# A later transpose of the gate, and other PSUM banks for two products of the output projection

## The chip, the cores and the metric

The kernel runs on one core of one Trainium2 chip, in one launch. The metric is the device time of an execution in microseconds (us). Three runs of the kernel before took 2272.88, 2274.70 and 2276.16 us; their median is 2274.7 us.

The engines are named as the profile names them: PE is TensorE (matmuls and transposes), PEld its weight loads, ACT is ScalarE, DVE is VectorE, POOL is GpSimd, and SP is the queue that issues most loads. PSUM, into which TensorE writes, has eight banks here, each a tile of 128 x 512 f32 values.

## The reference

One decoder block for 512 tokens of width 2048, in f32, batch 1:

```
mod = silu(c) @ w_ada + b_ada              # 2048 -> 6 x 2048
shift1, scale1, gate1, shift2, scale2, gate2 = split(mod, 6)
h = rms_norm(x, norm1_w) * (1 + scale1) + shift1
aq, ak, av, gq, gf, gi, gg = split(h @ w_in)      # seven times 1024 columns
attn = rms_norm(dilated_attention(rope(norm(aq)), rope(norm(ak)), av))   # 8 heads, 3 branches
hg   = rms_norm(hgrn2(gq, gf, gi)) * silu(gg)     # 8 heads of a gated linear recurrence
x = x + gate1 * (concat(attn, hg) @ w_out)        # w_out is 2048 x 2048
h2 = rms_norm(x, norm2_w) * (1 + scale2) + shift2
x = x + gate2 * (square(relu(h2 @ w_ff1)) @ w_ff2)   # 2048 -> 8192 -> 2048
```

## The kernel before

Every large matmul is done with numbers split into a high and a low part: `hi` and `lo` of the activations, `whi` and `wlo` of the weights. ScalarE casts the weights `wraw` to `whi` (L39), VectorE subtracts to get `wlo` (L40), and TensorE does three matmuls of 128 x 512 for each pair of tiles (`tok_mm`, L201 to L203, with tokens on the output's partitions; `ch_mm`, L209 to L211, with channels there).

A **product** is 512 columns of a projection. It holds four banks `prj`, one for each 128 rows of output, and runs over 16 slices of 128 of the inner dimension, so it has 16 steps of 12 matmuls. The input projection is a row of such products (`project`, about 180 to 800 us), the output projection has four (`project_out(q)`, q from 0 to 3, about 800 to 990 us). After a product ScalarE copies its four banks out: `gg` of the last product of the input projection at L711, in `hg_gate`; `x1` of the output projection at L944, in `residual`.

PSUM is one pool with two tags of four banks each, `bg` and `mm`: `bank(name, tag="bg")`. A tile gets a bank of its tag that has been given back, and waits for the instruction that reads the former tile last.

Small work is put between the matmul steps by generators. `tick()` takes one step of the list `tasks`: attention, the recurrence, and the turning of their results. `bg_step()` takes one step of the background list `bgw`, 1.85 of them for each step of a product of the input projection. The background work is the modulation `mod`: a step loads `araw`, 128 rows and 512 columns of `w_ada` (L125), and VectorE sums it up with the weights `sc` into `acc` (L129, L131); after the last load of 512 columns TensorE turns the sum into a column (`pc`, L151) and ScalarE reads that out (L154). `mod_rows(2, gate1)` does so for the four quarters of gate 1, lets `lag` background steps pass, turns the columns `gcol` into rows with one transpose (`pr`, L182), copies them (`row`, L184) and writes them to memory (L185), from where `gate1_bc` reads them (L914) after product 1. Behind it in the list stand the eight parts of scale 2 and shift 2 (`mod_cols`).

Attention of a head, in `attention`: `heads_t` turns queries and keys (`ptq`, L458); `scores` (`pscore`, L472, and on VectorE L478 to L481); `weights_t` turns the weights (`pT`, L494); `values` (`po`, L505), which VectorE reads out in four pieces (L509). Values of one head and scores of the next follow each other directly on TensorE. All these tiles, and `pc`, `pr` and the ones below, take banks of tag `bg`.

The output projection needs the results with channels on partitions. `to_mix` turns one head (`ptm`, four transposes of 128 x 128, L553), ScalarE reads it out with a weight (`mix`, L555), and `split_mix` splits that into `hi` (ScalarE, L242) and `lo` (VectorE, L243). In product 1 these run just ahead of the matmuls that need them. In products 2 to 4 and behind, `x1_transposed` turns the new `x1` (`pt2`, L931).

TensorE's order is the order in which the program is written from the input projection's third group on (`manual_schedule`). The order of the other engines is set by a scheduler with its own estimates of durations; a load or a copy marked high priority is put ahead.

Of the kernel before, what the change touches and what calls it, by code (L numbers as in the profile page):

```python
# [19 lines left out]
NT = S // P  # L20
# [24 lines left out]
def hybrid_block(ctx, tc, x, c, positions, norm1_w, w_ada, b_ada, w_in, q_norm_w, k_norm_w,  # L45
# [22 lines left out]
    def bank(name, tag="bg"):  # L68
        return ps.tile([P, 512], F32, name=name, tag=tag)
# [92 lines left out]
    def mod_cols(kind, b, dst, nw, n=512, early=False):  # L162

        for _ in gemv(ada_v, sc, kind * D + b * n, n, early):
            yield
        nb = n // P
        d = dst[:, b * nb:(b + 1) * nb]
        yield from to_cols(gemv.acc, d)
        dve.tensor_tensor(d, d, bcol[:, kind * NK + b * nb:kind * NK + (b + 1) * nb], op=ALU.add)
        if nw is not None:  # L170
            mod_cols.last = dve.scalar_tensor_tensor(d, d, 1.0, nw[:, b * nb:(b + 1) * nb], op0=ALU.add, op1=ALU.mult)
        yield

    def mod_rows(kind, dst, lag=3):

        col = gcol
        for b in range(4):
            yield from mod_cols(kind, b, col, None)
        for _ in range(lag):
            yield  # L180
        pr = bank("pr")
        pe.transpose(pr[0:NK, 0:P], col, ident)  # L182
        row = work("row")
        act.copy(row[0:NK, 0:P], pr[0:NK, 0:P])  # L184
        nc.sync.dma_start(dst.rearrange("o (r p) -> (o r) p", p=P), row[0:NK, 0:P])  # L185
        yield

    def load_w(view, k0, c0, n=512, eng=None, ahead=True, raws=None, behind=False):
        with tc.high_priority() if ahead else ExitStack():
            raw = wr.tile([P, 2, n], F32, name="wraw", tag="raw", bufs=4)  # L190
            with tc.issue_after(marks[-3].ins) if behind else ExitStack():
                nc.sync.dma_start(raw, view[:, k0:k0 + 2, c0:c0 + n])
            if raws is not None:
                raws[:] = [raw[:, 0], raw[:, 1]]
            return [_split(nc, wr, raw[:, j], n, eng if j else None) for j in range(2)]

    def tok_mm(banks, hi, lo, whi, wlo, first, last):

        for ti in range(NT):
            ts = slice(ti * P, (ti + 1) * P)  # L200
            pe.matmul(banks[ti], lhsT=hi[:, ts], rhs=whi, start=first, stop=False)  # L201
            pe.matmul(banks[ti], lhsT=hi[:, ts], rhs=wlo, start=False, stop=False)  # L202
            pe.matmul(banks[ti], lhsT=lo[:, ts], rhs=whi, start=False, stop=last)  # L203
# [30 lines left out]
    def work(name, dt=F32):  # L234
        return wk.tile([P, 512], dt, name=name, tag="wk")
# [113 lines left out]
    def bg_step():  # L349

        while bgw:
            try:
                return next(bgw[0])
            except StopIteration:
                bgw.pop(0)
# [3 lines left out]
    def tick(n=1):  # L359

        for _ in range(n):
            while tasks:
                try:
                    next(tasks[0])
                    break
                except StopIteration:
                    tasks.pop(0)
# [24 lines left out]
    def split_mix():  # L392

        if len(mixp) == NK or mix[korder[len(mixp)]] is None:
            return False
        mixp.append(pair(len(mixp)))
        split_to(mixp[-1], mix[korder[len(mixp) - 1]])
        return True
# [334 lines left out]
    later = []  # L733
    gate1 = dr.tile([1, D], F32, name="gate1")
    gate2 = dr.tile([1, D], F32, name="gate2")
    later.append(mod_rows(2, gate1))
    for b in range(4):
        later.append(mod_cols(4, b, g2c, n2c))
        later.append(mod_cols(3, b, s2c, None))
# [135 lines left out]


    def project_out(q, rate, after):
        banks = [bank("prj", tag="bg" if q % 2 and i < 2 else "mm") for i in range(4)]
        for i0 in range(0, NK, 2):
            for j, (whi, wlo) in enumerate(load_w(wout_v, korder[i0], q * 512)):  # L880
                i = i0 + j
                while q == 0 and len(mixp) <= i:
                    if not split_mix():
                        tick()
                while q == 0 and split_mix():
                    pass
                tok_mm(banks, *mixp[i], whi, wlo, i == 0, i == NK - 1)
                tick(2 if q == 0 and i < 10 else 1)
                owed[0] += rate
                while owed[0] >= 1.0:  # L890
                    bg_step()
                    owed[0] -= 1.0
                after(i)
        return banks

    def nothing(i):
        pass

    banks = project_out(0, 0, nothing)
    while tasks:  # L900
        tick()
# [38 lines left out]
    def residual(q, banks):  # L940
        qs_ = slice(q * 512, (q + 1) * 512)
        with tc.high_priority():
            for ti in (2, 3, 0, 1) if q % 2 else range(NT):
                act.copy(x1[ti][q], banks[ti])  # L944
        for ti in range(NT):
            t = x1[ti][q]
            dve.tensor_tensor(t, t, gate1_bc[:, qs_], op=ALU.mult)
            dve.tensor_tensor(t, t, xin[ti], op=ALU.add)
            act.activation(xin[ti], t, AF.Square, accum_out=ss2[:, ti, q:q + 1])
            pool.dma_start(x1d[:, ti, qs_], t)  # L950

    for q in range(4):
        xin = []
        for ti in range(NT):
            t = xr.tile([P, 512], F32, name="xin", tag="x")
            act.dma_start(t, x_t[:, ti, q * 512:(q + 1) * 512])
            xin.append(t)
        if q:
            banks = project_out(q, 1.7, u_split if q == 3 else nothing)
        residual(q, banks)  # L960
        tasks.append(x1_transposed(q, "bg" if q < 3 else "mm"))
# [221 lines left out]
    def product(i, src, c, ws, tag, by_tile, nxt):  # L1183


        banks = [bank("f2", tag=tag) for _ in range(2)]
        fh, fl = operand(src, c, i)
        ahead = []

        def mm(u, whi, wlo, ts_):  # L1190
            for a in range(2):
                for t in ts_:
                    ts = slice(t * P, (t + 1) * P)
                    first, end = u + a == 0, u + a == KG
                    pe.matmul(banks[t], lhsT=fh[u][a][:, ts], rhs=whi[:, a], start=first, stop=False)  # L1195
                    pe.matmul(banks[t], lhsT=fh[u][a][:, ts], rhs=wlo[:, a], start=False, stop=False)  # L1196
                    pe.matmul(banks[t], lhsT=fl[u][a][:, ts], rhs=whi[:, a], start=False, stop=end)  # L1197

        if by_tile:
            for t in range(2):  # L1200
                for u in range(KG):
                    mm(u, *ws[u], (t,))
        else:
            for u in range(KG):
                mm(u, *ws[u], range(2))
                if u == KG - 1 or src is hparts:
                    tick()
                if nxt and u < KG - 1:
                    ahead.append(nxt(u))
        return banks, ahead  # L1210
# [49 lines left out]
    def after(cs):  # L1260

        return {1: cs[5], 5: cs[6], 6: cs[1], 7: cs[7]}
# [78 lines left out]
    for item, following in zip(items, items[1:] + [None]):  # L1341
        stage_, blk, j, i = item
# [13 lines left out]
        if stage_ == 1:  # L1356
            banks, ahead = product(i, hparts, 0, ws, "bg" if first and j < 2 else "mm", False, call)
# [10 lines left out]
        else:  # L1368
            q, c = blk
            banks, ahead = product(i, fparts, c, ws, "mm", i == 2 and c == NC - 1, call)  # L1370
# [49 lines left out]
def _program(arrays):  # L1420
    import concourse.bacc as bacc
    nc = bacc.Bacc("TRN2", target_bir_lowering=False, num_devices=1)
    args = [nc.dram_tensor(n, a.shape, mybir.dt.from_np(a.dtype), kind="ExternalInput").ap()
            for n, a in arrays.items()]
    args.append(nc.dram_tensor("out_0_dram", _OUTS[0][0], F32, kind="ExternalOutput").ap())
    with tile.TileContext(nc, schedule_with_timeline_sim=True) as tc:
        hybrid_block(tc, *args)
    return nc
# [10 lines left out]
```

## Time and profile before

| | us |
|---|---|
| median of three runs | 2274.7 |
| the profiled execution | 2273.89 |
| its span, from the first to the last instruction | 2272.1 |
| TensorE busy with matmuls | 2219.7 |
| VectorE, ScalarE, GpSimd busy | 1809.6, 1097.3, 441.8 |

Matmuls are pipelined: one of 128 x 512 lasts 0.39 us in the trace, and the next one starts about 0.23 us after it. A row of the rows in time has the start in us from the span's start, the duration in us, the engine, the line, the operation, what it writes and reads, and in brackets the idle time of its engine before it, with what ended it. Several instructions of a kind that follow each other are one row, with their count. A row of waits has the engine and line that waited, what it waited for, and then the total in us, the number of times and the longest.

### The profile page before, as it was taken

What the parts mean: (1) busy time and instruction counts of PE and PEld (TensorE: products, weight loads), DVE (VectorE), ACT (ScalarE), POOL (GpSimd) and SP (SyncE); (2) the same over time, 40 slices, a digit from 0 to 9 for tenths busy, and PEclk for the clock granted to TensorE, in tenths of its full rate; (3) what the DMA queues carried; (4) which work ended last, traced back from release to release, by engine and by line L of the source; (5) the groups of instructions that cost most, each with busy time, mean ns of one, the idle gap of its engine ahead of it and who ended that gap; (6) DMA issues with size and microseconds to landing.
All of it is one profiled execution on the core that took longest, in us unless ns stands there. A gap on an engine that the chain in (4) does not pass through costs nothing.

```text
span 2272.1 us, 33110 instructions
## 1 busy us (share of the span) xinstructions
PE 2219.7 (98%) x11769; PEld 1821.1 (80%) x11769; DVE 1809.6 (80%) x2765; ACT 1097.3 (48%) x1950; POOL 441.8 (19%) x664
## 2 busy tenths in 40 slices
PE   4899999999999999999999999999999999999999
PEld 3788778888778888888887888888888888888887
DVE  6999878768786575678658988998897779967878
ACT  5555434443454464457544555565564333443332
POOL 1000022000220000003232323323232222222221
PEclk9999999999999999999999999999999999999999
DMA  9799454646555266747879789879889987998884
GB/s 324 255 335 336 139 177 150 214 149 211 170 178 160 71 227 202 267 120 264 322 280 361 274 306 385 297 290 377 319 294 378 358 310 263 349 347 310 305 295 164
DMA packets 262583, 598.32 MB, mean 263 GB/s; under 512 B 23220, under 2 KB 43968, under 8 KB 262416
## 3 DMA queue, kind: packets, MB, share of 16 engines
q1 hardware_dynamic: 186800, 332.54, 43.6%
q0 software_dynamic: 70720, 254.21, 30.4%
q10 hardware_dynamic: 4896, 9.44, 1.2%
q8 instruction: 93, 1.52, 0.3%
q14 instruction: 74, 0.61, 0.1%
HBM read 518.49 MB, written 77.61 MB: 262 GB/s over the span
## 4 chain that ended last, share of the span: by engine, by line
PE 70%; DMA 10%; DVE 8%; issue 8%; POOL 2%; ACT 1%; SPq 0%; POOLq 0%; DVEq 0%; ACTq 0%
PE f L1197 9%; PE f L1196 9%; PE f L1195 9%; PE prj L201 8%; PE prj L203 8%; PE prj L202 8%; DMA araw<-in_w_ada_dram 3%; PE f L211 2%; PE f L209 2%; PE f L210 2%; DVE vlo L1180 2%; DMA f_lod<-fs 2%; DVE raw L1163 2%; PE prj L209 1%; PE prj L210 1%
## 5 line engine op out<-in xcount | busy, mean ns | idle before, releaser
L1179 ACT CAST vhi<-raw 128x1024 fp32r<-128x1024 f32 x392 | 413.5, 1055 | 534.1 <-PE f L1197 419.4
L1180 DVE TENSOR_TENSOR vlo<-raw,vhi 128x1024 fp32r<-128x1024 f32 x392 | 476.3, 1221 | 150.8 <-ACT vhi L1179 150.0
L1196 PE MATMUL f<-vlo,Fh 128*128 128x512 f32 x1376 | 537.1, 390 | 3.4 <-DVE vlo L1180 3.3
L1197 PE MATMUL f<-vhi,Fl 128*128 128x512 f32 x1376 | 535.8, 389 | 0.5 <-DMA Fl<-f_lod 0.5
L1195 PE MATMUL f<-vhi,Fh 128*128 128x512 f32 x1376 | 536.1, 390 | 0.0
L39 ACT CAST whi<-wraw 128x512 fp32r<-128x512 f32 (+1 forms) x368 | 219.8, 601 | 445.9 <-PE prj L203 309.7
L201 PE MATMUL prj<-whi,hi 128*128 128x512 f32 x896 | 363.5, 406 | 1.3 <-ACT gg L711 1.3
L203 PE MATMUL prj<-whi,lo 128*128 128x512 f32 x896 | 350.6, 391 | 0.0
L202 PE MATMUL prj<-wlo,hi 128*128 128x512 f32 x896 | 350.0, 391 | 0.6 <-DVE wlo L40 0.6
L40 DVE TENSOR_TENSOR wlo<-wraw,whi 128x512 fp32r<-128x512 f32 (+1 forms) x368 | 243.3, 666 | 115.3 <-ACT whi L39 109.5
L131 DVE SCALAR_TENSOR_TENSOR acc<-araw,sc,acc 128x512 f32<-128x512 f32 (+1 forms) x392 | 254.0, 674 | 99.8 <-DMA araw<-in_w_ada_dram 98.6
L1196 PEld LDWEIGHTS f<-vlo,Fh 128*128 128x128 f32 x1376 | 258.3, 188 | 62.3 <-DVE vlo L1180 8.9
L1197 PEld LDWEIGHTS f<-vhi,Fl 128*128 128x128 f32 x1376 | 258.3, 188 | 54.2 <-DMA Fl<-f_lod 0.9
L1195 PEld LDWEIGHTS f<-vhi,Fh 128*128 128x128 f32 x1376 | 258.3, 188 | 53.7
L1163 DVE TENSOR_TENSOR raw<-raw,raw 128x1024 f32<-128x1024 f32 x224 | 268.3, 1218 | 3.5 <-DMA raw<-in_w_ff_dram 3.1
L203 PEld LDWEIGHTS prj<-whi,lo 128*128 128x128 f32 x896 | 168.1, 188 | 36.6 <-DVE lo L243 0.3
L201 PEld LDWEIGHTS prj<-whi,hi 128*128 128x128 f32 x896 | 168.3, 188 | 36.4 <-ACT gg L711 1.6
L202 PEld LDWEIGHTS prj<-wlo,hi 128*128 128x128 f32 x896 | 168.6, 188 | 33.5 <-DVE wlo L40 1.7
L1141 POOL DMA_DIRECT2D Fh<-f_hid x112 | 79.0, 705 | 424.0 <-PE f L1197 410.3
L211 PE MATMUL f<-hi,wlo 128*128 128x512 f32 x256 | 99.9, 390 | 1.2 <-DVE wlo L40 1.2
L209 PE MATMUL f<-hi,whi 128*128 128x512 f32 x256 | 100.3, 392 | 0.0
L210 PE MATMUL f<-lo,whi 128*128 128x512 f32 x256 | 99.6, 389 | 0.0
(311 smaller groups left out, 2912.0 us busy)
## 6 DMA issues: line engine op xcount, KB each, us to landing
raw<-in_w_ff_dram SPq DMA_DIRECT2D x224, 512.0 KB, 10.1
araw<-in_w_ada_dram SPq DMA_DIRECT2D x384, 256.0 KB, 4.3
Fh<-f_hid POOLq DMA_DIRECT2D x112, 512.0 KB, 6.7
Fl<-f_lod POOLq DMA_DIRECT2D x112, 512.0 KB, 7.8
wraw<-in_w_in_dram SPq DMA_DIRECT2D x104, 512.0 KB, 4.4
Fh<-h_hid POOLq DMA_DIRECT2D x60, 512.0 KB, 6.4
Fl<-h_lod POOLq DMA_DIRECT2D x60, 512.0 KB, 7.4
f_hid<-part POOLq DMA_DIRECT2D x48, 512.0 KB, 8.0
```

Of the source, the lines that this page charges most:

```text
L39: nc.scalar.copy(hi, src)
L40: (eng or nc.vector).tensor_tensor(lo, src, hi.bitcast(F32), op=ALU.subtract)
L131: dve.scalar_tensor_tensor(acc, raw[:, k - k0], vec[:, k:k + 1], acc, op0=ALU.mult, op1=ALU.add)
L201: pe.matmul(banks[ti], lhsT=hi[:, ts], rhs=whi, start=first, stop=False)
L202: pe.matmul(banks[ti], lhsT=hi[:, ts], rhs=wlo, start=False, stop=False)
L203: pe.matmul(banks[ti], lhsT=lo[:, ts], rhs=whi, start=False, stop=last)
L1163: dve.tensor_tensor(dst, a, b, op=ALU.subtract)
L1179: cast_done.append(act.copy(hi, src))
L1180: split_done.append(dve.tensor_tensor(lo, src, hi.bitcast(F32), op=ALU.subtract))
L1195: pe.matmul(banks[t], lhsT=fh[u][a][:, ts], rhs=whi[:, a], start=first, stop=False)
L1196: pe.matmul(banks[t], lhsT=fh[u][a][:, ts], rhs=wlo[:, a], start=False, stop=False)
L1197: pe.matmul(banks[t], lhsT=fl[u][a][:, ts], rhs=whi[:, a], start=False, stop=end)
```

## The change

Two edits, and a third that goes with the second. The lag between the columns of gate 1 and their transpose is six background steps, not three. The products that take two of their banks from tag `bg` are those with even q (the first and the third), not those with odd q. The copies out of the banks are written in the order of the token tiles for all products, where those of odd q had the order 2, 3, 0, 1.

```diff
@@ -733,7 +733,7 @@
     gate1 = dr.tile([1, D], F32, name="gate1")
     gate2 = dr.tile([1, D], F32, name="gate2")
-    later.append(mod_rows(2, gate1))
+    later.append(mod_rows(2, gate1, 6))
@@ -875,7 +875,7 @@
     def project_out(q, rate, after):
-        banks = [bank("prj", tag="bg" if q % 2 and i < 2 else "mm") for i in range(4)]
+        banks = [bank("prj", tag="bg" if q % 2 == 0 and i < 2 else "mm") for i in range(4)]
@@ -940,7 +940,7 @@
         with tc.high_priority():
-            for ti in (2, 3, 0, 1) if q % 2 else range(NT):
+            for ti in range(NT):
                 act.copy(x1[ti][q], banks[ti])
```

How this moves the instructions, at three places. First, TensorE in the input projection, at the transpose `pr` of gate 1 behind the scores of the second head (a piece of the difference):

```order
 L472 MATMUL pscore<-qT 128x128
 L472 MATMUL pscore<-qT 128x256
-L182 MATMUL pr<-ident,gcol 16x128
 L209 MATMUL prj<-hi_1018,whi 128x512
 L210 MATMUL prj<-lo_1019,whi 128x512
 L211 MATMUL prj<-hi_1018,wlo 128x512
+L182 MATMUL pr<-ident,gcol 16x128
 L209 MATMUL prj<-hi_1122,whi 128x512
```

The transpose stands one step of twelve matmuls later. Eight groups of `pc` behind it have moved by one or two steps as well.

Second, one of these groups, in the attention of the last four heads. On TensorE it stood behind the `ptq` before these values and scores, and stands now directly behind the scores. On VectorE, these rows led up to the reading of the values (L509) before:

```order
L131 SCALAR_TENSOR_TENSOR acc<-araw,sc,acc 128x512
L171 SCALAR_TENSOR_TENSOR g2c<-g2c,cols 128x4
L131 SCALAR_TENSOR_TENSOR acc<-araw,sc,acc 128x512 x2
L40 TENSOR_TENSOR wlo<-wraw,whi 128x512
L131 SCALAR_TENSOR_TENSOR acc<-araw,sc,acc 128x512
L509 TENSOR_SCALAR aq<-po,lsum 128x128 x4
```

and these do now:

```order
L40 TENSOR_TENSOR wlo<-wraw,whi 128x512
L481 TENSOR_SCALAR m<-m 128x1 x2
L507 RECIPROCAL lsum<-lsum 128x4
L40 TENSOR_TENSOR wlo<-wraw,whi 128x512 x5
L509 TENSOR_SCALAR aq<-po,lsum 128x128 x4
```

The sums `acc` of the background (L131) have moved away from this place.

Third, TensorE at the beginning of product 1 of the output projection, with what each instruction waits for; before:

```order
L201 MATMUL prj<-whi,hi_8701 128x512 [waits Activation_49]
L202 MATMUL prj<-wlo,hi_8701 128x512
L203 MATMUL prj<-whi,lo_8702 128x512
L553 MATMUL ptm<-ident,gg 128x128 [waits PE_49]
L553 MATMUL ptm<-ident,gg 128x128 x7
L553 MATMUL ptm<-ident,aq 128x128 [waits PE_49]
L553 MATMUL ptm<-ident,aq 128x128 x3
L201 MATMUL prj<-whi,hi_8728 128x512 [waits Activation_49]
```

and now:

```order
L201 MATMUL prj<-whi,hi_8701 128x512 [waits Activation_49]
L202 MATMUL prj<-wlo,hi_8701 128x512
L203 MATMUL prj<-whi,lo_8702 128x512
L553 MATMUL ptm<-ident,gg 128x128 [waits PE_49]
L553 MATMUL ptm<-ident,gg 128x128 x3
L553 MATMUL ptm<-ident,gg 128x128 [waits PE_49]
L553 MATMUL ptm<-ident,gg 128x128 x3
L553 MATMUL ptm<-ident,aq 128x128 [waits Activation_49]
L553 MATMUL ptm<-ident,aq 128x128 x3
L201 MATMUL prj<-whi,hi_8728 128x512
```

The order is the same, the banks are others: the product's first two tiles are in two `bg` banks, and the transposes `ptm` take turns on the other two, so that the third group waits for ScalarE's reading of the first. On ScalarE, the reading of the third group (`mix`, L555) has moved behind the next `hi` (L242) and the next `sg` (L715).

## The prediction

> **What bounds the kernel now.** I read the page's busy times and clock first, then the waits of TensorE, then the stretches of the program that the change touches, then the rows of time around each wait in them.
>
> ```profile
> PE 2219.7 (98%) x11769; PEld 1821.1 (80%) x11769; DVE 1809.6 (80%) x2765; ACT 1097.3 (48%) x1950; POOL 441.8 (19%) x664
> PEclk9999999999999999999999999999999999999999
> ```
>
> TensorE is busy for 2219.7 of 2272.1 us, and its clock is granted in full. A change can only give back TensorE's idle time, 52 us in all, and the next view says where that lies.
>
> ```profile
> PE pc L151 <- DVE acc L131: 12.9, 3, 11.9
> PE ptx L286 <- ACT xs L280: 12.4, 1, 12.4
> PE prj L209 <- ACT hi L339: 6.9, 3, 4.1
> PE pr L182 <- DVE aq L509: 1.6, 1, 1.6
> PE prj L201 <- ACT gg L711: 1.3, 1, 1.3
> ```
>
> The three large waits stand before 100 us, where the change moves nothing. Two small ones are in its reach: the transpose `pr` of gate 1 (1.6 us) and the first matmul of the output projection (1.3 us). Between them, and behind them, this is how full the engines are (busy time with the number of instructions for PE, PEld, DVE, ACT and POOL, then the granted clock and DMA):
>
> ```profile
> 460.00:780.00 320.00, 320.00 (x2365) 260.90 (x2364) 237.60 (x548) 136.01 (x397) 34.10 (x55) 1.00 0.52 161
> 780.00:820.00 40.00, 38.67 (x194) 31.93 (x194) 26.90 (x61) 28.14 (x57) 1.01 (x1) 1.00 0.32 99
> 820.00:990.00 170.00, 169.43 (x784) 139.63 (x783) 110.18 (x177) 75.66 (x162) 6.59 (x12) 1.00 0.70 231
> ```
>
> From 460 to 780 us TensorE has no idle time at all: whatever is reordered there can gain nothing, and can only use up slack. So the most that the change can bring is 1.6 + 1.3 us.
>
> **Part 1: `pr` three steps later.** It is one transpose, one ScalarE copy and one DMA of gate 1's row, and every later background step (the loads `araw`, the sums `acc`, the transposes `pc`) moves behind it by three steps.
>
> ```profile
> 439.63 2.32 PE L472 MATMUL pscore<-qT 128*128 128x512 f32 x8
> 441.66 0.75 DVE L131 SCALAR_TENSOR_TENSOR acc<-araw,sc,acc 128x512 f32<-128x512 f32 x1 [0.55 <-DMA araw<-in_w_ada_dram]
> 442.33 1.12 DVE L509 TENSOR_SCALAR aq<-po,lsum 128x128 f32<-128x128 f32 x4
> 443.50 0.28 PE L182 MATMUL pr<-ident,gcol 128*16 128x128 f32 x1 [1.55 <-DVE aq L509]
> 443.54 0.48 PE L209 MATMUL prj<-hi,whi 128*128 128x512 f32 x1
> ```
>
> The scores end at 439.63 + 2.32 = 441.95. `pr` needs a bank that the values product `po` has held, and VectorE reads it out until 442.33 + 1.12 = 443.45. The order now puts twelve matmuls ahead of `pr`. Twelve matmuls take 2.86 us (800.84 to 803.70 below), so `pr` is reached at about 444.8, over 1 us after its bank is free. The 1.55 us go: **-1.55**. Its copy and its DMA come 3 us later, and that row is read back only when product 1 is over:
>
> ```profile
> L914 SPq DMA_DIRECT2D gate_bc<-gate x4: 319/374/977, 837.0 to 841.8; - x4
> ```
>
> That costs nothing.
>
> What moves with it: eight groups of `pc` come one or two matmul steps later. The only one that comes to stand where `pr` stood, right behind values and scores, is that of the next head group:
>
> ```profile
> 711.90 2.39 PE L505 MATMUL po<-av,p_sb 128*128 128x128 f32 x20
> 712.10 0.62 ACT L39 CAST whi<-wraw 128x512 fp32r<-128x512 f32 x1 [0.77 <-PE prj L203]
> 714.13 2.32 PE L472 MATMUL pscore<-qT 128*128 128x512 f32 x8
> 714.39 0.68 DVE L40 TENSOR_TENSOR wlo<-wraw,whi 128x512 fp32r<-128x512 f32 x1
> 715.13 0.75 DVE L131 SCALAR_TENSOR_TENSOR acc<-araw,sc,acc 128x512 f32<-128x512 f32 x1
> 715.80 1.12 DVE L509 TENSOR_SCALAR aq<-po,lsum 128x128 f32<-128x128 f32 x4
> 716.10 0.59 PE L201 MATMUL prj<-whi,hi 128*128 128x512 f32 x1
> ```
>
> With the group gone from ahead of this place TensorE is 0.35 us earlier, at its scores' end near 715.7. Were VectorE to read `po` out when it does now, until 716.92, `pc` would wait 1.2 us: the wait of part 1 would only have moved. But its order has changed too: the sums `acc` that stood around this point have moved on, and the four reads stand directly behind a `wlo`. That `wlo` needs a `whi` that is cast from about 711.8 on, and so ends near 713; `po` itself ends near 714 (711.90 + 2.39 less 0.35). The reads then run to about 714 + 1.12 = 715.1, ahead of 715.7. I take **0**, with 0 and +1.2 as the bounds. The other moves of loads, casts and sums fall in the stretch without idle time, and there the weights are ready well ahead:
>
> ```profile
> ACT whi L39 <- PE prj L203: 309.7, 154, 6.5
> ```
>
> Here the cast of the next weights waits for TensorE to give a buffer back, 154 times: ScalarE is ahead, not behind. **0**.
>
> **Part 2: banks of the output projection.** Product 1 now takes two banks of tag `bg`, so its first six matmuls need not wait until `gg` has been copied out of the four `mm` banks. TensorE, then ScalarE, around that place:
>
> ```profile
> 798.91 0.60 PE L553 MATMUL ptm<-ident,gg 128*128 128x128 f32 x4
> 800.84 0.50 PE L201 MATMUL prj<-whi,hi 128*128 128x512 f32 x1 [1.33 <-ACT gg L711]
> 803.70 1.03 PE L553 MATMUL ptm<-ident,gg 128*128 128x128 f32 x8
> 804.57 0.60 PE L553 MATMUL ptm<-ident,aq 128*128 128x128 f32 x4
> 804.92 0.48 PE L201 MATMUL prj<-whi,hi 128*128 128x512 f32 x1
> 807.77 1.04 PE L553 MATMUL ptm<-ident,aq 128*128 128x128 f32 x8
> 808.56 0.48 PE L201 MATMUL prj<-whi,hi 128*128 128x512 f32 x1
> 811.59 1.04 PE L553 MATMUL ptm<-ident,aq 128*128 128x128 f32 x8
> ```
>
> ```profile
> 800.21 2.04 ACT L711 COPY gg<-prj 128x512 f32<-128x512 f32 x4
> 802.62 1.19 ACT L715 ACTIVATE sg<-gg 128x512 f32<-128x512 f32 x2
> 803.89 0.62 ACT L39 CAST whi<-wraw 128x512 fp32r<-128x512 f32 x1
> 804.42 1.26 ACT L555 ACTIVATE mix<-ptm,cols 128x512 f32<-128x512 f32 x2
> 806.60 0.69 ACT L555 ACTIVATE mix<-ptm,cols 128x512 f32<-128x512 f32 x1
> 809.26 1.27 ACT L555 ACTIVATE mix<-ptm,cols 128x512 f32<-128x512 f32 x2
> 815.43 0.63 ACT L39 CAST whi<-wraw 128x512 fp32r<-128x512 f32 x1 [0.83 <-PE prj L203]
> ```
>
> Four transposes hold TensorE for 0.35 us (804.57 to 804.92), so the product could begin at 798.91 + 0.35 = 799.26 and not at 800.84: **-1.58**. Its third bank is reached 1.5 us later, at 800.8, just when the first copy of `gg` ends (800.21 + a quarter of 2.04 = 800.7, plus some 0.1): no new wait there.
>
> But the price stands one step on. Three groups of transposes (`ptm`) follow the first twelve matmuls back to back. Before, four banks served them; now the product holds two for its whole length and they take turns on two, so the third group needs the first one's bank. Walking it: the product begins at 799.26, its twelve matmuls end at 802.12, two groups take 0.87 (803.70 to 804.57) to 802.99. The first is read out by ScalarE's `mix` at 804.42, and ScalarE is not free earlier by much: copies, then `sg` until 802.62 + 1.19 = 803.81, then the `whi` cast, which today starts at 803.89 as its buffer comes free and could start at about 803.75. So `mix` runs from 804.28 to 804.28 + 0.68 = 804.96 (the single one at 806.60 took 0.69), and the third group starts there, ends at 805.31, where today the next matmul starts at 804.92. The new wait is 804.96 - 802.99 = **+1.97**; part 2 sums to 1.97 - 1.58 = **+0.39**. Bounds: with ScalarE exactly as now, `mix` ends at 805.10 and the sum is +0.53; with no new wait it is -1.58.
>
> From there on the two banks suffice: each later step has one pair of transposes, and the pair of 807.77 is read out by 809.26 + 1.27 = 810.53, 1.06 us before the next pair begins at 811.59, so I take 0, with what rival D says as the upper end.
>
> Products 2 to 4: no TensorE idle time stands at their starts, so nothing can be gained, and the copies are early enough in either order of banks:
>
> ```profile
> 895.21 2.63 ACT L944 COPY x<-prj 128x512 f32<-128x512 f32 x4
> ```
>
> Copies follow the last matmuls of their banks; the last ends at 897.84, while the next product begins near 897.2 and reaches its third bank 1.5 us and its fourth 2.2 us later. The edit of the order in `residual` moves nothing: in the built programs the copies stand as token tile 0, 1, 2, 3 in both. Product 3 shares the other two `bg` banks with the turned tiles `pt2` as product 2 does today without a wait. **0**.
>
> **Sum.** -1.55 + 0 + 0.39 + 0 = -1.16 us. Span 2272.1 becomes 2270.9, and with the 1.8 us around it the profiled execution's 2273.9 becomes 2272.7. That execution was 0.8 us under the median of the runs, so the forecast for the median is 2274.7 - 1.2 = **2273.5**.
>
> **Rivals.** B: the new wait at the third transposes does not come. For it speaks that ScalarE's `mix` may be put off only by casts that the scheduler places; against it, that its order there is unchanged up to that `mix`. Then -1.55 - 1.58: 2271.6. C: the wait of part 1 comes back at the `pc` of 715 us. For it: the same three things stand in the same order as at 443 us. Against: the sums moved away from ahead of the reads. Price +1.2: 2274.7. D, the other side: ScalarE falls behind on the two banks. One `mix` has moved behind an `hi` cast and an `sg`, 1.05 us later in its queue, and if each of the next four pairs of transposes waits about 1 us for its bank, 4 us are added: 2277.5. It decides once a pair is read out more than the roughly 1 us of slack late; against it speaks that ScalarE has caught up by 815.43, where it waits 0.83 us for TensorE. E: the granted clock falls. The 1.33 us idle time in 780 to 820 left it at 1.00, and a wait of 1.97 us is not much longer.
>
> The Trainium skill (TensorE: Matmul & The Clock Gate, on psum-queue depth-cycling) tells of a kernel that cycled through PSUM banks with small idles and lost its full clock again and again, which speaks against two banks in turn. By its half rate the 192 matmuls of this product, at 0.24 us each, would take some 46 us more, and the time would be about 2320. The trace so far does not bear it out, since the clock stood at 1.00 through the stretch that holds the wait of 1.33 us.
>
> **How the numbers follow.** Chances: the forecast 0.58, B 0.12, C 0.15, D 0.09, E and things not named 0.06. The likeliest's own range, with the spread of the runs (2272.9 to 2276.2), is 2271.8 to 2275.3. The stated range reaches down past B and up to D: 2270.4 to 2277.3. 0.2% is 4.5 us, about what a measurement of this kernel can tell from no change. Neither B (-3.1) nor D (+2.8) reaches it, so only the last case and the outer edge of D or B do: faster 0.05, same 0.89, slower 0.06.
>
> **What would show it.** In the profile after: no row of `pr` waiting for `aq`; no wait of `prj` L201 for `gg` L711; a new row in which `ptm` L553 waits some 2 us for `mix` L555, once, near 803 us; no wait of `pc` L151 for `aq` L509. A `pc` that waits near 714 us shows C; several waits of `ptm` show D; no such row shows B. I am wrong as a whole if TensorE's idle time changes by over 3 us, or in the stretch from 460 to 780 us, where I say that nothing is lost.

## The result: slower by 0.2%, lost at a place that no edit touches

The changed kernel takes 2279.2 us in the median (22 runs, 2275.7 to 2284.1), the kernel before 2274.4 us (22 runs on the same chip). The ratio is 1.0021, with a 95% interval of 1.0014 to 1.0027: 4.8 us slower, where 1.2 us faster was forecast, and above the upper end of the range. The profiled execution took 2281.47 us, its span 2279.6.

TensorE's waits after:

```profile
PE ptx L286 <- ACT xs L280: 13.0, 1, 13.0
PE pc L151 <- DVE acc L131: 13.0, 2, 12.6
PE prj L209 <- ACT hi L339: 7.1, 4, 4.1
PE pB L583 <- DVE z L610: 5.7, 3, 3.6
PE ptm L553 <- ACT mix L555: 1.6, 1, 1.6
```

What was forecast is there: the waits of `pr` for `aq` and of the first `prj` for `gg` are gone, and `ptm` waits once for `mix`. New is the fourth row. `pB` belongs to the recurrence (`hgrn_head`): 32 small matmuls that take `z`, which VectorE makes (L609, L610). None of this is in the diff. The stretches of the program after, in the columns of the view before:

```profile
460.00:540.00 80.00, 79.89 (x576) 65.40 (x575) 61.14 (x135) 29.00 (x71) 0.53 (x1) 1.00 0.57 178
540.00:620.00 80.00, 78.98 (x737) 63.13 (x736) 63.59 (x144) 31.00 (x103) 13.97 (x27) 1.00 0.56 176
620.00:700.00 80.00, 76.43 (x598) 61.26 (x597) 61.62 (x138) 36.88 (x123) 19.28 (x27) 0.96 0.55 170
700.00:780.00 80.00, 79.94 (x410) 66.28 (x409) 52.07 (x129) 36.64 (x94) 0.76 (x1) 1.00 0.37 112
780.00:820.00 40.00, 38.41 (x199) 32.02 (x198) 20.88 (x47) 24.20 (x51) 1.01 (x1) 1.00 0.22 69
```

From 460 to 780 us TensorE had no idle time before. Now 4.8 us of it are idle (0.11 + 1.02 + 3.57 + 0.06), and in 620 to 700 the granted clock is 0.96. The same place in slices of 2 us:

```profile
620.00:622.00 2.00, 1.85 (x9) 1.18 (x7) 0.00 (x0) 0.11 (x1) 0.00 (x0) 1.00 0.27 90
622.00:624.00 2.00, 0.00 (x0) 0.00 (x0) 0.86 (x2) 0.50 (x1) 0.00 (x0) 1.00 0.01 2
624.00:626.00 2.00, 0.58 (x32) 0.52 (x33) 2.00 (x8) 0.00 (x0) 0.00 (x0) 0.68 0.48 125
626.00:628.00 2.00, 2.00 (x12) 1.62 (x6) 2.00 (x7) 0.00 (x0) 0.00 (x0) 0.50 0.78 214
628.00:630.00 2.00, 2.00 (x6) 1.53 (x5) 1.97 (x6) 0.00 (x0) 0.00 (x0) 0.50 0.14 54
630.00:632.00 2.00, 2.00 (x7) 1.62 (x6) 1.97 (x8) 0.47 (x1) 0.00 (x0) 0.61 0.22 23
632.00:634.00 2.00, 2.00 (x11) 1.57 (x9) 1.96 (x6) 1.81 (x7) 0.96 (x2) 1.00 0.66 240
```

TensorE waits, and then runs for 6.8 us at half its clock (0.68, 0.50, 0.50 and 0.61 in slices of 2 us) while its busy time reads 2.00 of 2.00. To see what that costs I paired the weight matmuls of the two traces one by one, since their number and order are the same, and followed how far each starts later than its partner. The change makes 2.0 us good at `pr`, loses 1.1 at 579 us, 3.4 at 621 us in one step and 3.0 more in the next 6 us, wins 1.6 at 801 us and loses 2.0 at 805 us. The rest of the difference of 7.4 us at the end is in places that the change does not touch (1.2 us at 338 us, for one, where `pB` waits 1.1 us ahead of everything that the lag moves).

Why `z` was late. The loads on the page, then SyncE's queue, VectorE and TensorE in time:

```profile
araw<-in_w_ada_dram SPq DMA_DIRECT2D x384, 256.0 KB, 4.4
```

```profile
618.40 0.33 SPq L125 DMA_DIRECT2D araw<-in_w_ada_dram  x1
```

```profile
617.62 0.75 DVE L131 SCALAR_TENSOR_TENSOR acc<-araw,sc,acc 128x512 f32<-128x512 f32 x1 [1.39 <-DMA araw<-in_w_ada_dram]
618.29 0.69 DVE L40 TENSOR_TENSOR wlo<-wraw,whi 128x512 fp32r<-128x512 f32 x1
623.14 0.75 DVE L131 SCALAR_TENSOR_TENSOR acc<-araw,sc,acc 128x512 f32<-128x512 f32 x1 [4.17 <-DMA araw<-in_w_ada_dram]
623.81 0.28 DVE L624 TENSOR_TENSOR mt<-pA,hgm 128x128 f32<-128x128 f32 x1
624.01 0.41 DVE L609 TENSOR_TENSOR z<-kk,Sx 128x256 f32<-128x256 f32 x1
624.95 0.42 DVE L610 TENSOR_TENSOR z<-gq,f 128x256 f32<-128x256 f32 x1
```

```profile
621.46 0.39 PE L203 MATMUL prj<-whi,lo 128*128 128x512 f32 x1
625.42 0.65 PE L583 MATMUL pB<-z 128*32 128x32 f32 x32 [3.57 <-DVE z L610]
```

A background sum of the modulation (`acc`, L131), which nobody needs soon, stands ahead of `z` on VectorE, and VectorE works in order. Its load goes out at 618.40, when the sum of 617.62 gives back its buffer: in the built program both loads use the same one of the four `araw` buffers. From issue to landing a load takes 4.4 us in the median of 384 (the last number of the row from the page's part on DMA issues), so the sum stands still for 4.17 us with `z` behind it. Before, this was the same place:

```profile
613.83 0.33 SPq L125 DMA_DIRECT2D araw<-in_w_ada_dram  x1
616.86 0.75 DVE L131 SCALAR_TENSOR_TENSOR acc<-araw,sc,acc 128x512 f32<-128x512 f32 x1 [2.46 <-DMA araw<-in_w_ada_dram]
618.33 0.42 DVE L609 TENSOR_TENSOR z<-kk,Sx 128x256 f32<-128x256 f32 x1
619.26 0.42 DVE L610 TENSOR_TENSOR z<-gq,f 128x256 f32<-128x256 f32 x1
```

A sum waited 2.46 us for its load here too, but ended early enough: `pB` came at 620.40, without a wait, 0.7 us after `z` was done (619.26 + 0.42). The three empty steps have moved the loads and sums against the recurrence, and used up this slack. Two parts of that can be read off the rows. The load went out 6.6 us before TensorE came to `pB` (613.83 to 620.40), and goes out 3.5 us before it now (618.40 to 621.85, which is 625.42 less the wait). And from issue to the start of its sum it took 3.0 us before and 4.7 us now. So some 3 us are the shift, and 1.7 us are that this load was slower than its partner.

### The profile page after: what moved, and what is told of

Its sections match the earlier page's. It is cut to its first block, busy times and chain, and to the rows that moved or that the text cites. A ratio compares the mean times of both kernels' runs of the same rounds, so it can differ in the third digit from the quotient of the medians.

```text
span 2279.6 us, 33100 instructions
## 1 busy us (share of the span) xinstructions
PE 2221.6 (97%) x11769; PEld 1823.5 (80%) x11769; DVE 1810.5 (79%) x2765; ACT 1098.0 (48%) x1950; POOL 442.3 (19%) x664
## 4 chain that ended last, share of the span: by engine, by line
PE 68%; DVE 13%; DMA 10%; issue 5%; ACT 2%; POOL 1%; SPq 0%; DVEq 0%; POOLq 0%; ACTq 0%
PE f L1196 10%; PE f L1197 10%; PE f L1195 10%; PE prj L201 7%; PE prj L203 6%; PE prj L202 6%; DMA araw<-in_w_ada_dram 4%; DVE vlo L1180 3%; DVE raw L1163 2%; PE f L211 2%; PE f L209 2%; PE f L210 2%; PE prj L209 2%; PE prj L210 2%; PE prj L211 2%
## 5 line engine op out<-in xcount | busy, mean ns | idle before, releaser
L131 DVE SCALAR_TENSOR_TENSOR acc<-araw,sc,acc 128x512 f32<-128x512 f32 (+1 forms) x392 | 254.4, 675 | 104.9 <-DMA araw<-in_w_ada_dram 103.8
```

The source lines that it names most:

```text
L131: dve.scalar_tensor_tensor(acc, raw[:, k - k0], vec[:, k:k + 1], acc, op0=ALU.mult, op1=ALU.add)
```

## The experiments

All were run beside the kernel before. Median and ratio of each against it:

| | median, before's | ratio, interval | longest wait of `pB` |
|---|---|---|---|
| lag 6 alone | 2280.9, 2275.2 | 1.0026 [1.0015, 1.0038] | 2.7 |
| banks alone | 2275.5, 2275.2 | 1.0001 [0.9992, 1.0009] | none |
| lag 6, third `acc` | 2285.1, 2275.2 | 1.0036 [1.0022, 1.0050] | 2.2 |
| lag 6, fifth `araw` | 2273.6, 2275.2 | 0.9998 [0.9989, 1.0007] | 1.6 |
| lag 6, one load less | 2277.1, 2274.4 | 1.0002 [0.9993, 1.0011] | 1.2 |
| lag 5 alone | 2278.5, 2274.4 | 1.0019 [1.0009, 1.0028] | 3.6 |
| lag 3, fifth `araw` | 2272.0, 2274.4 | 0.9987 [0.9978, 0.9996] | 1.1 |
| one bank for product 1 | 2275.3, 2274.4 | 1.0003 [0.9993, 1.0013] | none |
| `pr` moved alone | 2272.9, 2274.8 | 0.9991 [0.9982, 0.9999] | none |
| loads moved alone | 2281.1, 2274.8 | 1.0027 [1.0018, 1.0036] | 2.8 |
| the change, fifth `araw` | 2274.2, 2274.8 | 0.9997 [0.9988, 1.0006] | 2.9 |
| `pr` alone, fifth `araw` | 2270.6, 2274.8 | 0.9980 [0.9972, 0.9989] | 1.4 |

### The two edits apart

```diff
-    later.append(mod_rows(2, gate1))
+    later.append(mod_rows(2, gate1, 6))
```

> Only the first edit of the change (the gate's transpose six steps behind its columns); banks and residual order as before. Theory (the sums that stand ahead of the recurrence's z on VectorE wait for a late load, TensorE then waits 3.6 us at pB and runs at a clock of 0.50 for some 6 us): about +4.4 us against the kernel before (-1.6 at pr, +3.4 wait, +3 clock, some tenths elsewhere), and the profile has PE pB L583 <- DVE z L610 at about 621 us with some 3.6 us and a granted clock near 0.5 just behind it. Rival (the loss is with the banks of the output projection): -1.6 us, and no such wait. Second rival (the loss at 621 us is of that one execution only): -1.6 us on the median, the wait in some profiles and not in others.

The other, with the copies of `residual` in plain order:

```diff
-        banks = [bank("prj", tag="bg" if q % 2 and i < 2 else "mm") for i in range(4)]
+        banks = [bank("prj", tag="bg" if q % 2 == 0 and i < 2 else "mm") for i in range(4)]
```

> Only the second edit of the change (products 1 and 3 take two banks of the other set, residual copies in plain order); the transpose stays three steps behind. Theory: +0.4 us against the kernel before (product 1 starts 1.6 us earlier, its third ptm group waits some 2.0 us for mix), no wait at pB, the pr wait for aq of 1.6 us still there. Rival (the loss is with the banks): +4 to +6 us.

The lag makes the whole loss (1.0026), the banks make none that can be measured (1.0001). With the lag alone `pB` waits 2.7 us at this place and the clock falls again, for 3.4 us this time. Slices of 2 us:

```profile
622.00:624.00 2.00, 0.91 (x33) 0.85 (x34) 2.00 (x8) 0.00 (x0) 0.00 (x0) 0.70 0.56 142
624.00:626.00 2.00, 2.00 (x6) 1.52 (x6) 2.00 (x6) 0.00 (x0) 0.00 (x0) 0.50 0.78 225
626.00:628.00 2.00, 2.00 (x10) 1.67 (x9) 1.97 (x7) 0.10 (x1) 0.00 (x0) 0.95 0.07 26
```

That profile holds a second loss, of 2.6 us in the paired matmuls: at 1240 us `pt` (L1225) waits 1.86 us for VectorE, and the clock falls there too. The changed kernel's profile has 0.98 us at `pt` and no fall, so what this has to do with the lag is not shown.

In the profile of the banks alone both rows forecast for them stand side by side, `ptm` new and `pr` as ever:

```profile
PE ptm L553 <- ACT mix L555: 1.6, 1, 1.6
PE pr L182 <- DVE aq L509: 1.4, 1, 1.4
```

Paired, product 1 begins 1.8 us earlier there and its third `ptm` group comes 2.0 us later: +0.2, where the forecast had +0.39.

### Is it the transpose, or the loads that move with it?

Two kernels, each with half of what the lag does. In the first `pr` stands where six steps put it, but the steps of the next block of columns stay where they were, and none of them is put off by empty ones. TensorE's order differs from before in the place of `pr` alone.

```diff
-    def mod_rows(kind, dst, lag=3):
+    def mod_rows(kind, dst, lag=3, rest=None):
...
-        for _ in range(lag):
+        for n in range(lag + 3 if rest else lag):
+            if rest and n > 3: next(rest)
             yield
...
-        yield
+        yield from rest or (None,)
...
-    later.append(mod_rows(2, gate1))
+    later.append(mod_rows(2, gate1, 3, mod_cols(4, 0, g2c, n2c)))
     for b in range(4):
-        later.append(mod_cols(4, b, g2c, n2c))
+        if b: later.append(mod_cols(4, b, g2c, n2c))
```

> The gate's transpose alone is moved to where six steps put it, and nothing else: the three background steps behind the third are not left empty but are steps of the next block of columns, so all loads and sums keep the place that they have in the kernel before. Theory (the later transpose gains what was forecast, and the loss is from the loads and sums that the three empty steps push back): -1.6 us against the kernel before, no wait at pr, none over 1 us at pB at 579 and 621 us. Rival (the late transpose itself makes the loss, by its bank or by the write of the gate): +4 to +6 us.

In the second `pr` stays, and the three empty steps stand behind it:

```diff
-        yield
+        yield from [None] * (4 if kind == 2 else 1)
```

> The other half: the transpose stays three steps behind, and three empty background steps stand behind it, so all later loads and sums are pushed back as with six steps. Theory: the wait of 1.6 us at pr stays and the loss at 579 and 621 us comes as with six steps: +4 to +6 us against the kernel before, some 1.6 us more than the first edit alone, with a wait of 1 to 4 us at pB at 621 us that differs from one execution to the next with the landing of one load. Rival (empty steps cost nothing, TensorE has no idle time there): 0 us.

The transpose alone: 0.9991, 1.9 us under the kernel before. The loads alone: 1.0027, 6.3 us above it. The intervals are far apart, and the waits say the same. Moving `pr` alone leaves no row of `pr` and none of `pB`, and TensorE full again:

```profile
540.00:620.00 80.00, 80.00 (x774) 63.81 (x773) 64.73 (x149) 32.15 (x110) 15.27 (x27) 1.00 0.57 179
620.00:700.00 80.00, 80.00 (x595) 64.43 (x593) 63.60 (x140) 39.67 (x127) 19.93 (x27) 1.00 0.58 178
```

Moving the loads alone has both:

```profile
PE pB L583 <- DVE z L610: 4.5, 3, 2.8
PE pr L182 <- DVE aq L509: 1.5, 1, 1.5
```

So what the edit was written for fits what it was forecast to be worth, and the loss comes with the three empty steps.

### Is it the one late load?

The sum ahead of `z` at 621 us is that of row block 6 in the third quarter of shift 2. Here its load is left out (lag 6; so shift 2 is computed from wrong rows there):

```diff
-            raw = spare.pop(0) if early and spare else slot("araw") if early else gv.tile([P, 512], F32, name="araw", bufs=4)
-            raw = raw.rearrange("p (k n) -> p k n", n=n)
-            asked[0] = nc.sync.dma_start(raw, view[:, k0:k0 + nk, col0:col0 + n])
+            load = not (view is ada_v and col0 == 3 * D + 1024 and k0 in (6,)); raw = raw if not load else spare.pop(0) if early and spare else slot("araw") if early else gv.tile([P, 512], F32, name="araw", bufs=4)
+            raw = raw.rearrange("p (k n) -> p k n", n=n) if load else raw
+            if load: asked[0] = nc.sync.dma_start(raw, view[:, k0:k0 + nk, col0:col0 + n])
```

> The first edit alone (six steps), and one load left out: the sum of row block 6 in the third block of the second shift (the one that stands ahead of z at 621 us) takes the rows of block 4 again and so waits for no load of its own; the instructions of VectorE and TensorE stand in the same order around it. So g2's shift is computed from wrong rows there, and the time is that of one 256 KB load less. Theory (that load's lateness is the whole cause): no wait over 0.5 us at pB at 621 us, the granted clock stays at 1.00 behind it, and the time is 4.5 to 5.5 us under the first edit alone, so -0.5 to +0.5 us against the kernel before (the wait of 1.2 us at 579 us stays). Rival (VectorE is simply too busy there with the sums, loads or not): a wait of 2 us or more stays, and at least half of the loss.

One thing in this text was wrong: the block loaded just before is 5, not 4, so the sum takes the rows of block 5 and still waits for that load, which goes out one buffer earlier. VectorE, then TensorE, then the clock behind it:

```profile
617.76 0.75 DVE L131 SCALAR_TENSOR_TENSOR acc<-araw,sc,acc 128x512 f32<-128x512 f32 x1 [1.04 <-DMA araw<-in_w_ada_dram]
619.57 0.42 DVE L610 TENSOR_TENSOR z<-gq,f 128x256 f32<-128x256 f32 x1
```

```profile
620.04 0.46 PE L583 MATMUL pB<-z 128*32 128x32 f32 x32 [0.87 <-DVE z L610]
```

```profile
620.00:622.00 2.00, 1.96 (x39) 1.67 (x40) 2.00 (x8) 0.00 (x0) 0.00 (x0) 1.00 0.48 111
622.00:624.00 2.00, 2.00 (x11) 1.65 (x10) 1.97 (x7) 0.52 (x1) 0.00 (x0) 1.00 0.40 152
```

The wait is 0.87 us here (the 1.2 of the table ends at 338 us), not the 0.5 us or less that I expected, and the clock stays at 1.00. The ratio falls from 1.0026 to 1.0002, and the two intervals do not meet. The median by itself, 2.7 us above that of the kernel before, shows a smaller gain than the ratio, so its size is not fixed to better than some 2 us. The profiled execution (2271.9 us) was also the fastest of the 11, 5.2 us under their median, so the rows show this place at its best and not how the others fared. VectorE's work is the same, so it is the standing still that costs here, and not the work.

### What holds the buffers?

My theory said that the odd sums of a block, which wait for the second `acc`, hold three of the four `araw` buffers. Two kernels with lag 6, both with one buffer less in the work pool to make room:

```diff
-    gv = pk.enter_context(tc.tile_pool(name="gv", bufs=2))
+    gv = pk.enter_context(tc.tile_pool(name="gv", bufs=3))
```

> The first edit alone, with a third buffer for acc (the room comes from one buffer less in the work pool, 8 to 7); TensorE's order of instructions is that of the first edit alone. Theory (the odd sums of a block of columns can't begin before the pc of the block before has read its acc, so their loads hold three of the four araw buffers and the even sums run through one): with a third acc the loads go out earlier, the wait at pB falls under 1 us and the granted clock stays at 1.00 behind 621 us: about -1.6 us against the kernel before, some 6 us under the first edit alone. Rival (the place of the sums ahead of z is all that counts, not the buffers): as the first edit alone, +4.4 us with the wait of 3.6 us.

```diff
-            raw = spare.pop(0) if early and spare else slot("araw") if early else gv.tile([P, 512], F32, name="araw", bufs=4)
+            raw = spare.pop(0) if early and spare else slot("araw") if early else gv.tile([P, 512], F32, name="araw", bufs=5)
```

> The first edit alone, with a fifth buffer for araw (the room again from the work pool, 8 to 7). Theory (the last load ahead of z goes out only when a sum frees its buffer, at 618.3 us, and lands 4.7 us later): one load more is in flight, so the sum ahead of z finds its data earlier; the wait at pB falls to 0 to 1.5 us, no slow clock behind it, -1.6 to 0 us against the kernel before. Rival (the buffers of the loads are not it; the odd sums wait for acc): +4.4 us as the first edit alone, since the fifth buffer is held by a further odd load.

The third `acc` missed: 2285.1 us, slower than the lag alone. VectorE's order changed in about a hundred places, TensorE now waits 4.51 us for a `pc` at 236 us, and at the place in question a sum still stands still ahead of `z`:

```profile
630.54 0.75 DVE L131 SCALAR_TENSOR_TENSOR acc<-araw,sc,acc 128x512 f32<-128x512 f32 x1 [3.66 <-DMA araw<-in_w_ada_dram]
```

The odd sums of the block still come only behind the `pc` of the block before (`pc` at 640.86, the first of them at 644.66), so the third buffer did not do what it was meant to do, and the theory about `acc` was not put to the test. Half of it can be read from the trace of the lag alone: the loads issued at 608.49, 612.23 and 614.74 us have no sum before 635.53, so three of the four buffers are held at this place. What holds their sums back, `acc` or VectorE's order, stays open. The fifth `araw` reaches 0.9998, with 1.6 us as the longest wait of `pB`. The load that was late leaves at 612.04 here, not at 617.21 as with the lag alone, and its sum (615.12) no longer waits. But one sum more now stands ahead of `z`, and that one stands still for 3.23 us:

```profile
615.12 0.75 DVE L131 SCALAR_TENSOR_TENSOR acc<-araw,sc,acc 128x512 f32<-128x512 f32 x1
619.71 0.75 DVE L131 SCALAR_TENSOR_TENSOR acc<-araw,sc,acc 128x512 f32<-128x512 f32 x1 [3.23 <-DMA araw<-in_w_ada_dram]
621.99 0.46 PE L583 MATMUL pB<-z 128*32 128x32 f32 x32 [1.39 <-DVE z L610]
```

That last sum ends 1.1 us earlier than the late one with the lag alone, `pB` waits 1.39 us, and the clock stays at 1.00. VectorE's order changed in some 180 places here, and the smaller work pool was not run by itself, so that the buffer alone makes the gain is likely and not shown. This execution (2272.2 us) was the second fastest of 11.

### Other lags, and the fifth buffer elsewhere

Lag 5 (`mod_rows(2, gate1, 5)`):

> Only the lag, five steps in place of three or six. Theory (the loss hangs on whether a late load's sum stands ahead of a z that is due, that is on the phase of the loads against the recurrence, not on the transpose itself): the wait at pr falls by some 1.6 us as with six; at 621 us two sums or more stand between the block's first and z in place of one, and the wait there is under 2 us, too short for the clock to fall: -1.5 to +0.5 us against the kernel before. Rival (any lag over three makes the same loss): +4 to +6 us.

A miss: 1.0019, and the wait is there in full, 3.6 us at `pB`. I had counted how many sums stand between the block's first and `z`; that count does not tell when the load lands. Lag 5 and lag 6 lose alike; lag 4 was not run.

The fifth buffer at lag 3 (the kernel before with that edit):

> The kernel before (three steps, its banks), with the fifth araw buffer alone (room from the work pool, 8 to 7). Theory (a fifth buffer takes the waits for late loads out where they set TensorE's wait; at three steps there are none but the pr wait): within 1 us of the kernel before, and the pr wait of 1.6 us stays. Rival (the fifth buffer is worth some 6 us by itself, whatever the lag): -5 us or more.

It is 2.4 us faster than the kernel before, between the two theories. `pr` still waits 1.2 us. Part of the gain stands at 1265 us in the trace, where `f` no longer waits 1.5 us for `vlo`; why it does not, and whether the smaller work pool has a part in it, was not taken apart. The profiles of lag 6 and lag 5 alone lack this wait as well, without a fifth buffer.

The whole change with the fifth buffer:

> The whole change with a fifth araw buffer (room from the work pool, 8 to 7). Theory (the fifth buffer takes the loss at 621 us away as it did for the first edit alone; the banks cost 0.4 us): -1.5 to +0.5 us against the kernel before, some 5 us under the change. Rival (the two edits together lose elsewhere too): +2 us or more.

0.9997: the median is 5 us under that of the change. The profiled execution (2278.8 us, 4.6 above the median) had a wait of 2.90 us at `pB` at 579 us in place of 621. So with a fifth buffer a load can still land late.

### Product 1 with one bank of the other set

```diff
-        banks = [bank("prj", tag="bg" if q % 2 and i < 2 else "mm") for i in range(4)]
+        banks = [bank("prj", tag="bg" if (q % 2 and i < 2) or (q == 0 and i < 1) else "mm") for i in range(4)]
```

> Three steps; the banks of the kernel before, and product 1 takes one bank of the other set in place of none (products 2 and 4 two, as before). Theory (product 1 needs the first mm bank late by 1.5 us, and the transposes of mix need three banks of that set): product 1 starts some 1.5 us earlier and the third ptm group finds its bank free, no wait of 1.8 us for mix: -1 to -1.5 us against the kernel before. Rival (the fourth product's matmuls wait instead, or the start of product 1 is set by its weights): 0 to +0.5 us.

1.0003, a miss. TensorE at the beginning of product 1:

```profile
800.35 0.50 PE L201 MATMUL prj<-whi,hi 128*128 128x512 f32 x1 [0.63 <-ACT gg L711]
808.68 0.50 PE L203 MATMUL prj<-whi,lo 128*128 128x512 f32 x1 [0.59 <-DVE lo L243]
```

No `ptm` waits, as expected. But the 1.6 us won at the start are given back: the second bank still waits 0.63 us for `gg`, and two steps on TensorE waits 0.59 us for a `lo` of `mix`. With the banks dealt out like this, the splitting of `mix` sets the next wait.

### A version that beats both

`pr` moved alone, with the fifth `araw`:

> A version that may beat both: the transpose alone moved, loads in their old place, the banks of the kernel before, and the fifth araw buffer. Theory (the gains of the moved transpose, 1.3 to 1.6 us, and of the fifth buffer at three steps, 2.4 us, add, since they are in different places): -3.5 to -4 us against the kernel before. Rival (with the transpose gone from its place the same TensorE time is lost to the next wait there): -2.4 us, as with the fifth buffer alone.

2270.6 us against 2274.8, 0.9980 [0.9972, 0.9989]: 4.2 us under the kernel before, and by the medians some 8.6 under the changed one. The gains measured apart (1.9 and 2.4) add up to 4.3, so they fit a sum.

## Why the prediction was wrong, step by step

**`pr` three steps later: right.** -1.55 forecast; moved alone it measures -1.9 in the median, and the paired matmuls step by 1.9 to 2.0 us there (0.26 of which come back where `pr` now stands).

**`pc` at 715 us: right.** No row of `pc` waits for `aq`; of the bounds 0 and +1.2 the lower came.

**"The other moves of loads, casts and sums fall in the stretch without idle time ... 0": this step failed.** Forecast 0, measured +6.3 us for these moves alone; in the paired matmuls of that kernel's profile 5.2 of them lie between 573 and 627 us. I had read "no idle time" as "nothing to gain", which is right, and said that such a stretch "can only use up slack", but looked for slack at the weights only. What had to be looked at was each thing TensorE waits for there, `z` first of all: which sums stand ahead of it on VectorE, how long these stand still for their loads (2.46 us already before, in the rows above), and how early `z` was (0.7 us). The stall had no row in TensorE's waits, as it was still just covered.

**Product 1: right.** -1.58 and +1.97 forecast; -1.6 and +2.0 measured in the paired matmuls, of which the wait of `ptm` itself is 1.59 us. Rivals B and D did not come.

**Rival E, the clock, was put at the wrong place.** The 1.6 us wait of `ptm` left it at 1.00 in 780 to 820 us. It fell behind the wait that I had not seen, and nearly doubled its price. Nor is the clock "granted in full" before: in and behind the 4.06 us wait of `prj` for `hi` L339 (it ended at 94.4 us) it stood at half for 6.8 us, which the page's slices of 57 us do not show. Such a fall could have been priced from the trace. The Trainium skill (TensorE: Matmul & The Clock Gate, on how HAM oscillation bites in real kernels) names this form too, a wait for a DMA that lets the clock fall. I had weighed only the section behind it, on cycling through banks, which no run here shows.

**The sign of "I am wrong as a whole" was right**: lost time in 460 to 780 us.

**Two small slips in the range.** The forecast with the spread of the runs gives 2271.7 to 2275.0, not 2271.8 to 2275.3, and rival D's 2277.5 lies just above the stated upper end of 2277.3.

## What to carry to other kernels

A lag made of empty steps moves everything queued behind it; if one instruction is to come later, fill its place with the next work, so that nothing else moves. Where an engine works in order, look ahead of each urgent instruction for one that waits for a load: such a stall may stand in the trace without costing anything, and any shift of phase can expose it. In a full stretch of the bounding engine a row "waits for nothing" says nothing on how close the next wait is, so compare when the operand is ready with when it is used.

## What the runs showed of the hardware

Behind a wait of TensorE for `z` of 2.01, 2.16, 2.70, 2.81, 2.90, 3.57 or 3.61 us in the recurrence the granted clock fell to 0.50 or 0.51; behind 0.87, 1.39, 1.44 and 1.64 us there, and 1.59 us at `ptm`, it stayed at 1.00. But it also stayed at 1.00 behind 2.07 us, in the change with the fifth `araw`:

```profile
340.40 0.46 PE L583 MATMUL pB<-z 128*32 128x32 f32 x32 [2.07 <-DVE z L610]
```

```profile
342.00:344.00 2.00, 2.00 (x10) 1.63 (x10) 1.97 (x6) 0.14 (x1) 0.00 (x0) 1.00 0.58 217
```

And it fell behind 1.85 us at `pt`, with lag 5:

```profile
1240.37 0.44 PE L1225 MATMUL pt<-ident,s 128*128 128x128 f32 x2 [1.85 <-DVE s L1244]
```

```profile
1242.00:1244.00 2.00, 2.00 (x10) 1.90 (x9) 1.25 (x2) 1.74 (x3) 0.00 (x0) 0.50 1.06 388
```

With one bank for product 1 it stayed at 1.00 behind 1.82 us at the same place. So in these profiles a wait of some 1.8 to 2.1 us can go either way, and its length alone does not decide.

Behind waits of 1.85 to 2.90 us the clock was at half for 3.4 us, behind 3.57 and 3.61 us for 6.8 us (but behind the 4.51 us at `pc` for 3.4 us). In the 6 us behind a wait at 579 or 621 us the paired weight matmuls fell back by another 1.6 to 2.0 us where it had been 2.16 to 2.90 us long, by some 3 with 3.6 us, and by 0.4 with 0.9 to 1.4 us. So the slow clock costs 1 to 2.5 us on top of such a wait. The Trainium skill (TensorE: Matmul & The Clock Gate, on HAM oscillation) gives gaps over about 3.4 us as what to avoid; here less was enough, as in the row above and in these:

```profile
632.00:634.00 2.00, 1.18 (x35) 1.04 (x36) 2.00 (x8) 0.00 (x0) 0.00 (x0) 0.94 0.69 150
634.00:636.00 2.00, 2.00 (x6) 1.51 (x6) 2.00 (x7) 0.00 (x0) 0.00 (x0) 0.50 0.70 243
```

(Slices of the kernel with lag 6 and a third `acc`; the wait of 2.16 us ended at 632.82.) In four programs with the loads shifted by the lag the wait at 621 us was 2.70, 2.81, 3.57 and 3.61 us. That fits the changed kernel's spread of 8 us between its fastest and slowest run, but no two executions of one program were profiled, so that this spread comes from the landing of that load is likely and not shown.
